# Products over 64 rows in place of 128 in half of a projection stage

## The chip, the core and the metric

The kernel runs on one core of one Trainium2 chip. The core has TensorE (PE for its products, PEld for its weight loads), VectorE (DVE), ScalarE (ACT), GpSimd (POOL) and SyncE (SP), a working memory of 128 partitions, and an accumulation memory (PSUM) in banks of 512 fp32 numbers per partition, of which the kernel uses all eight here. The metric is device time in microseconds (us) of one execution; lower is better.

## The reference

Two layers of an encoder over 2048 prompt tokens and 64 new ones, 1024 wide, 16 heads of 64. What matters here is the four-way and the two-way projection at the head of each layer:

```python
def a_project(x, g, w_in):
    h = rms_norm(x, g)
    q, k, v, gate = jnp.split(h @ w_in, 4, axis=-1)
    return split_heads(q), split_heads(k), split_heads(v), gate

def b_project(x, g, w_in):
    h = rms_norm(x, g)
    q, gate = jnp.split(h @ w_in, 2, axis=-1)
    return split_heads(q), gate

def shared_kv(x, g, w_kv):
    h = rms_norm(x, g)
    k, v = jnp.split(h @ w_kv, 2, axis=-1)
    return split_heads(k), split_heads(v)

def gated_out(o, gate, w_out):
    b, t = o.shape[:2]
    return (o.reshape(b, t, D_MODEL) * jax.nn.silu(gate)) @ w_out
```

Layer a then attends within a band of 64-token chunks with a softmax, layer b over all earlier tokens with a stick-breaking rule; each ends in `gated_out` and a residual, and a last norm follows. All inputs and outputs are fp32.

## The kernel before

**Numbers in two parts.** Every operand of a product is kept as a high part in fp32r and a low part that is the rest, and a product of two such operands is three products: high by high, high by low, low by high. `mm3` (line 227) does this: over the eight blocks of 128 input channels (`NK` = 8) it issues 24 matmuls into one bank. `split` (line 209) makes the two parts out of a bank: ACT copies it to fp32r, DVE subtracts that copy from the bank.

**The stages of the program.** Layer a: `projections` (line 239), then band attention with its output projection; layer b: `projections` again, then stick-breaking attention with its output projection. In the trace the two projection stages lie at about 0 to 800 us and 1500 to 2030 us.

**Inside `projections`.** First come the values (`ps_v`), token rows as output. Then the part that matters here: for each job (`q`, `k` or `g`, the gate) and each pair of heads (`hp`, eight of them) the weights of 128 output channels are loaded (`wraw`), scaled and split into `wh` and `wl`, and multiplied with the normed, transposed tokens. These lie in two places: the first 1088 (1024 prompt tokens and the 64 new ones) in `x_own`, high and low, and the second 1024 prompt tokens in the pair of tiles `big`. `HALVES` (line 57) cuts the first half in chunks of 364, 362 and 362 columns and the second (`hf` = 1) in two of 512. Each chunk is one `mm3` into one bank `ps_t` (line 395); the banks of this stage are five, under the tag `mm`, taken in turn. Gates leave the bank through a SiLU on ACT (`sg`), queries and keys through `split` (`sh`, `sl`), and DMAs store them.

**What is left for later.** `DEFER` (line 42) takes the second half of the keys out of layer a's stage and the second half of queries and gates out of layer b's. So the second half is projected here for 16 cases in layer a (`q` and `g`, eight pairs of heads each) and 8 in layer b (`k`), with two chunks each: 48 chunks, 1152 matmuls.

**What sets the order.** Most of the program is ordered by a scheduler that places instructions on the engines at build time; in parts of the attention the order is written out by hand (`Beat`). Work on caches and biases (`stages`) and the transposes that turn keys back to token rows (`natural`, bank `ps_n`; `stage_cache`, bank `ps_c`) is spread between the projections, in three further banks. Each engine then runs its own list in order.

All instructions are recorded through one helper, so all of them stand under line 90 in the profile; the tiles' names tell them apart.

Of the kernel before, what the change touches and what calls it, by code (L numbers as in the profile page):

```python
# [9 lines left out]
F32 = mybir.dt.float32  # L10
F32R = mybir.dt.float32r
AF = mybir.ActivationFunctionType
ALU = mybir.AluOpType
# [3 lines left out]
P = 128  # L17
D = 1024
NK = D // P
H = 16  # L20
DH = 64
# [11 lines left out]
CH = 512  # L33
# [27 lines left out]
def spot(r):  # L61

    return (0, NEW) if r == NP else divmod(r, HALF)
# [7 lines left out]
def f32(ap):  # L71
    return ap.bitcast(F32)
# [28 lines left out]
def encoder_step(ctx: ExitStack, tc: tile.TileContext, a: dict, o: dict):  # L101
    nc = tc.nc
    order = InOrder(tc)
    dve, act, gps, pe = (order.engine(x) for x in (nc.vector, nc.scalar, nc.gpsimd, nc.tensor))
    mm = pe.matmul
# [66 lines left out]
    for L, rows in (("a", CACHE_A), ("b", PAST)):  # L172
# [4 lines left out]
            k=[dram.tile([2, P, T + rows], F32R, name=f"k_{L}{i}") for i in range(HP)],  # L177
# [6 lines left out]
            w={x: dram.tile([2, P, NK, P], F32R, name=f"w_{L}{x[0]}{x[1]}") for x in DEFER[L] if L in KEPT},  # L184
# [24 lines left out]
    def split(hi, lo, src):  # L209
        act.activation(hi, src, AF.Copy)  # L210
        dve.tensor_tensor(lo, src, f32(hi), ALU.subtract)

    def scaled_split(hi, lo, src, g):
        for k in range(src.shape[1]):
            act.activation(hi[:, k], src[:, k], AF.Copy, scale=g[:, k : k + 1])
            dve.scalar_tensor_tensor(lo[:, k], src[:, k], g[:, k : k + 1], f32(hi[:, k]), ALU.mult, ALU.subtract)
# [10 lines left out]
    def mm3(out, sh, sl, mh, ml):  # L227
        for k in range(NK):
            mm(out, sh(k), mh(k), start=(k == 0), stop=False)
            mm(out, sh(k), ml(k), start=False, stop=False)  # L230
            mm(out, sl(k), mh(k), start=False, stop=(k == NK - 1))

    def put(L, kind, hp, s, cols, part, by=nc.sync.dma_start):

        for i in (0, 2) if kind == "q" and s == 0 else (s,):
            by(f32(lay[L][kind][hp][i, :, cols]), f32(part))


    def projections(L, x_of, begin, w_v, cv, gv, out_v, jobs, first, prompt, sample, stages):
        with (  # L240
# [7 lines left out]
            with tc.tile_pool(name=f"v_{L}", bufs=2) as pool:  # L248
# [54 lines left out]
                for half in range(2):  # L303
                    wh, wl = [], []
# [17 lines left out]
                    for i, t in enumerate(seq):  # L322
# [3 lines left out]
                        hf, c = spot(r0)  # L326
                        xh, xl = xs[hf]
                        ps = psum.tile([P, CH], F32, name="ps_v", tag="mm", bufs=5)
                        out = ps[:n]
                        if n == NS:  # L330
# [4 lines left out]
                            out = pool.tile([P, CH], F32, name="vn", tag="vn", bufs=2)[:n]  # L335
# [30 lines left out]
            with tc.tile_pool(name=f"st_{L}", bufs=5) as spool, tc.tile_pool(name=f"t_{L}", bufs=2) as pool:  # L366
                for j, (kind, w, c0, g) in enumerate(jobs):
                    for hp in range(HP):
                        for _ in range(-(-len(stages) // (len(jobs) * HP - j * HP - hp))):
                            stages.pop(0)(pool)  # L370

                        home, tag = (pool, "wr") if hp % 2 else (opool, "og")
                        raw = home.tile([P, NK, P], F32, name="wraw", tag=tag, bufs=1)
                        c = c0 + hp * P
                        wh = opool.tile([P, NK, P], F32R, name="wh", tag="oh", bufs=2)
                        wl = opool.tile([P, NK, P], F32R, name="wl", tag="ol", bufs=2)

                        with tc.issue_after(first_copy.ins) if j == 0 and hp < 2 else nullcontext():
                            nc.scalar.dma_start(raw, w[:, c : c + P].rearrange("(k p) c -> p k c", p=P))
                            scaled_split(wh, wl, raw, g)  # L380
                        if (kind, hp) in lay[L]["w"]:
                            for i, part in enumerate((wh, wl)):
                                nc.sync.dma_start(f32(lay[L]["w"][kind, hp][i]), f32(part))
                        for hf, (r0, n, chunks) in enumerate(HALVES):
                            xh, xl = xs[hf]
                            if hf and (kind, hp) in DEFER[L]:

                                continue
                            if kind == "g":
                                sg = spool.tile([P, 1088], F32, name="sg", tag="st")  # L390
                            else:
                                sh = spool.tile([P, 1088], F32R, name="sh", tag="st")
                                sl = spool.tile([P, 1088], F32R, name="sl", tag="st")
                            for c, m in chunks:
                                ps = psum.tile([P, CH], F32, name="ps_t", tag="mm", bufs=5)
                                mm3(
                                    ps[:, :m],
                                    lambda k: wh[:, k],
                                    lambda k: wl[:, k],
                                    lambda k: xh[:, k, c : c + m],  # L400
                                    lambda k: xl[:, k, c : c + m],
                                )
                                if kind == "g":
                                    act.activation(sg[:, c : c + m], ps[:, :m], AF.Silu)
                                else:
                                    split(sh[:, c : c + m], sl[:, c : c + m], ps[:, :m])
                            if kind == "g":
                                nc.sync.dma_start(lay[L]["g"][hp][:, r0 : r0 + n], sg[:, :n])
                                continue
                            for s, part in enumerate((sh, sl)):  # L410
                                put(L, kind, hp, s, slice(r0, r0 + n), part[:, :n])
                            if kind == "k":

                                cols = slice(hp * P, hp * P + P)
                                for c in range(0, HALF, CH):
                                    b = hf * HALF + c - first
                                    if b >= 0:
                                        kf = pool.tile([P, CH], F32, name="kf", tag="kf", bufs=2)
                                        part = slice(c, c + CH)
                                        gps.tensor_tensor(kf, f32(sh[:, part]), f32(sl[:, part]), ALU.add)  # L420
                                        natural(pool, kf, 0, P, 4, prompt[b : b + CH, cols])
                                if hf == 0:
                                    kf = pool.tile([P, CH], F32, name="kf", tag="kf", bufs=2)
                                    part = slice(NEW, NEW + NS)
                                    gps.tensor_tensor(kf[:, :NS], f32(sh[:, part]), f32(sl[:, part]), ALU.add)
                                    natural(pool, kf, 0, NS, 1, sample[:, cols])
# [82 lines left out]
    def natural(pool, kf, at, n, nt, dst):  # L509
        ps = bank("ps_n").rearrange("p (j c) -> p j c", j=4)  # L510
        for j in range(nt):
            flip(ps[:n, j], kf[:, at + j * n : at + j * n + n])
        kn = pool.tile([P, 4, P], F32, name="kn", tag="kn", bufs=2)
        act.activation(kn[:n, :nt], ps[:n, :nt], AF.Copy)
        nc.sync.dma_start(dst.rearrange("(j p) c -> p j c", p=n), kn[:n, :nt])
# [220 lines left out]
    def late_job(L, kind, w, c0, g, hp, x2, first, prompt):  # L736
# [27 lines left out]
        def out(c):  # L764
            ps = st["ps"]
            at = slice(place(HALF + c), place(HALF + c) + CH)
            if kind == "g":
                sg = opool.tile([P, CH], F32, name="sg", tag="xr", bufs=2)
                act.activation(sg, ps, AF.Sigmoid)
                dve.tensor_tensor(sg, ps, sg, ALU.mult)  # L770
                queue.store(lay[L]["g"][hp][:, at], sg)
            else:
                sp = opool.tile([P, 2, CH], F32R, name="sp", tag="xr", bufs=2)
                split(sp[:, 0], sp[:, 1], ps)
                for s in range(2):
                    put(L, kind, hp, s, at, sp[:, s], queue.store)
                st[c] = sp
            if c + CH == HALF:
                done_late.add((L, kind, hp))
# [307 lines left out]
    with (  # L1087
# [158 lines left out]
        ("q", a["w_in_b"][0], 0, gs["b"]),  # L1246
    ]
    x2 = projections(
        "b",
        x1_rows,  # L1250
# [12 lines left out]
    with (  # L1263
# [9 lines left out]
            out=own_s[:, CH - P :], in_=own_s[:, CH - P :], pattern=[[-1, P]], compare_op=ALU.is_gt,  # L1273
# [3 lines left out]
        for h in range(2):  # L1277
            rows = slice(h * DH, h * DH + DH)
# [267 lines left out]
```

## Time and profile before

| what | value |
|---|---|
| median of 2 runs | 3279.51 us (3278.79 and 3280.22) |
| span of the profiled execution | 3278.2 us |
| what lies around the span, by the two runs | 0.6 to 2.0 us |
| PE busy | 3204.2 us, 98% of the span |
| PEld, DVE, ACT, POOL busy | 85%, 58%, 52%, 39% |
| mean granted TensorE clock | 0.994 of full speed |

A group of instructions is written as line, engine, operation, output<-inputs, rows*columns of the weights, shape, count, then busy time and mean duration of one, then the idle time of the engine before them. A product's duration holds its way through the array, so products overlap: the pace is read from the distance between starts. In a timeline, rows of like neighbours are merged: start, time from the first start to the last end, and a count.

### The profile page before, as it was taken

Reading aid. Unit: us, or ns where it says so; the run is one execution under the profiler, and the core shown is the slowest. Engines: PE = TensorE matmul, PEld = TensorE weight load, DVE = VectorE, ACT = ScalarE, POOL = GpSimd, SP = SyncE. Lnnn points to the kernel's source line nnn. Section 1 sums busy time; section 2 is a strip of 40 time slices with the busy share of each in tenths; the row PEclk is TensorE's granted clock in tenths of the full one; section 3 lists DMA queues with packets and bytes.
Section 4 is the critical chain, followed back from the end, with each engine's and each line's share of the span. In section 5 each row is a group of like instructions: output and inputs, shape, how many; then the busy total and the mean of one; then the engine's idle time right before and its main releaser. Section 6 shows DMA issues by size and latency. Waiting matters only on the chain.

```text
span 3278.2 us, 53687 instructions
## 1 busy us (share of the span) xinstructions
PE 3204.2 (98%) x17928; PEld 2791.0 (85%) x17928; DVE 1887.0 (58%) x3786; ACT 1711.4 (52%) x3719; POOL 1291.4 (39%) x1950
## 2 busy tenths in 40 slices
PE   8999999999998999999999999999999989999999
PEld 7889999988887898878889998788888878888877
DVE  4235431147778775231044333788878878888873
ACT  5234222258888776143134442566666656666662
POOL 3001110026665554020044200444477766877761
PEclk9999999999999999999999999999999999999999
DMA  6359993387899983553399999977735566455423
GB/s 202 121 185 368 349 331 118 117 237 220 240 260 267 252 237 130 164 174 128 113 357 352 348 357 328 251 217 217 213 121 148 162 203 174 124 143 141 138 72 119
DMA packets 464892, 688.41 MB, mean 210 GB/s; under 512 B 51446, under 2 KB 261398, under 8 KB 464615
## 3 DMA queue, kind: packets, MB, share of 16 engines
q1 hardware_dynamic: 405158, 633.85, 61.8%
q10 hardware_dynamic: 59456, 51.13, 4.8%
q8 instruction: 143, 2.34, 0.3%
q14 instruction: 135, 1.10, 0.1%
HBM read 408.78 MB, written 276.07 MB: 209 GB/s over the span
## 4 chain that ended last, share of the span: by engine, by line
PE 75%; issue 7%; DVE 6%; DMA 6%; ACT 2%; POOL 2%; SPq 1%; POOLq 0%; ACTq 0%; DVEq 0%
PE ps_t L90 23%; PE ps_v L90 11%; PE acc L90 10%; PE z L90 9%; PE wt L90 8%; PE ps_j L90 6%; PE ps_o L90 5%; DVE s L90 3%; DVE pl L90 2%; DMA vt<-v_b 1%; PE ps_tr L90 1%; ACT ph L90 1%; DMA kt<-k_b 1%; POOL s L90 1%; ACT s L90 1%
## 5 line engine op out<-in xcount | busy, mean ns | idle before, releaser
L90 DVE TENSOR_TENSOR pl<-wt,ph 128x512 fp32r<-128x512 f32 (+1 forms) x864 | 551.9, 654 | 122.4 <-ACT ph L90 118.7
L90 ACT ACTIVATE ph<-wt 128x512 fp32r<-128x512 f32 (+1 forms) x864 | 485.7, 578 | 205.4 <-PE wt L90 178.2
L90 PE MATMUL ps_t<-x_own,wh 128*128 128x362 f32 (+1 forms) x2304 | 567.5, 327 | 0.0
L90 PE MATMUL wt<-ident,s 128*128 128x128 f32 x3472 | 551.5, 274 | 13.4 <-DVE pl L90 6.8
L90 PEld LDWEIGHTS wt<-ident,s 128*128 128x128 f32 x3472 | 418.6, 141 | 88.3 <-DVE pl L90 12.9
L90 ACT ACTIVATE f<-z 128x512 f32<-128x512 f32 (+4 forms) x680 | 355.1, 535 | 196.1 <-PE z L90 139.7
L90 PEld LDWEIGHTS ps_t<-x_own,wh 128*128 128x128 f32 x2304 | 405.0, 188 | 1.8
L90 POOL TENSOR_TENSOR s<-f,s 128x256 f32<-128x256 f32 x416 | 361.3, 870 | 104.2 <-DVE s L90 95.9
L90 PE MATMUL acc<-ph,vt 128*128 128x512 f32 (+3 forms) x1088 | 376.2, 381 | 14.1 <-DMA vt<-v_b 7.5
L90 PE MATMUL z<-kt,q 128*128 128x512 f32 (+3 forms) x1280 | 375.4, 381 | 12.9 <-DMA q<-q_b 5.8
L90 PE MATMUL ps_t<-x_own,wl 128*128 128x362 f32 (+1 forms) x1152 | 376.7, 327 | 0.0
L90 PE MATMUL acc<-pl,vt 128*128 128x512 f32 (+3 forms) x1088 | 364.6, 368 | 7.2 <-DVE pl L90 6.8
L90 POOL TENSOR_SCALAR s<-s,rc 128x640 f32<-128x640 f32 (+5 forms) x264 | 199.2, 760 | 387.3 <-DMA keys<-k_a 193.3
L90 PE MATMUL ps_o<-big,oh 128*128 128x512 f32 x1088 | 336.2, 392 | 0.2 <-ACT oh L90 0.2
L90 POOL TENSOR_TENSOR two<-f 128x256 f32<-128x256 f32 x416 | 259.5, 626 | 166.3 <-ACT f L90 150.0
L90 DVE TENSOR_TENSOR_SCAN s<-two,s,own 128x256 f32<-128x256 f32 x408 | 299.7, 738 | 33.6 <-POOL two L90 32.3
L90 PEld LDWEIGHTS z<-kt,q 128*128 128x128 f32 x1280 | 221.9, 192 | 43.5 <-ACT f L90 11.8
L90 PE MATMUL ps_j<-big,lwh 128*128 128x512 f32 x768 | 246.9, 397 | 1.1 <-DVE pl L90 0.6
L90 PE MATMUL ps_t<-big,wh 128*128 128x512 f32 x768 | 238.9, 391 | 0.0
L90 PEld LDWEIGHTS ps_o<-big,oh 128*128 128x128 f32 x1088 | 202.2, 188 | 41.3 <-ACT oh L90 0.4
L90 PEld LDWEIGHTS acc<-ph,vt 128*128 128x128 f32 x1088 | 198.7, 192 | 37.1 <-ACT ot L90 8.4
L90 DVE CUSTOM_DVE_ANT_0 s<-z,bias 128x640 f32<-128x640 f32 (+4 forms) x256 | 184.7, 733 | 77.2 <-PE wt L90 51.1
(148 smaller groups left out, 5528.9 us busy)
## 6 DMA issues: line engine op xcount, KB each, us to landing
vt<-v_b SPq DMA_DIRECT2D x80, 512.0 KB, 4.9
v_b<-vs SPq DMA_DIRECT2D x64, 512.0 KB, 5.7
q<-q_a SPq DMA_DIRECT2D x128, 256.0 KB, 5.9
q<-q_b SPq DMA_DIRECT2D x128, 256.0 KB, 4.6
vt<-v_a SPq DMA_DIRECT2D x48, 512.0 KB, 7.1
kt<-k_b SPq DMA_DIRECT2D x96, 256.0 KB, 5.6
keys<-k_a SPq DMA_DIRECT2D x80, 256.0 KB, 7.1
v_a<-vs ACTq DMA_DIRECT2D x32, 512.0 KB, 2.7
```

The source lines that it names most:

```text
L90: ins = op(*args, **kwargs)
```

## The change

For chunks of the second half (`hf` = 1), and only there, `mm3` is replaced by the new `by_rows`. It takes a second bank of the same five and issues each of the 24 products as two: one over partitions 0 to 63 of weights and tokens into the first bank, one over partitions 64 to 127 into the second. Weights are still 128 columns wide and tokens 512. When both sums are done, ACT copies the first bank to a tile in working memory (`total`, under the tag `kf` that the keys use too) and DVE adds the second bank to it. What followed reads `total` in place of the bank: SiLU for gates, `split` for queries and keys. The 48 chunks so have 2304 matmuls in place of 1152, 48 more ACT and 48 more DVE instructions; loads and stores are the same in number and size.

```diff
+    def by_rows(pool, psum, ps, wh, wl, xh, xl):
+
+        outs = [ps, psum.tile([P, CH], F32, name="ps_t", tag="mm", bufs=5)]
+        terms = [(w, x, k) for k in range(NK) for w, x in ((wh, xh), (wh, xl), (wl, xh))]
+        for i, (w, x, k) in enumerate(terms):
+            for r, out in enumerate(outs):
+                rows = slice(r * DH, r * DH + DH)
+                mm(out, w[rows, k], x[rows, k], start=(i == 0), stop=(i == len(terms) - 1))
+        total = pool.tile([P, CH], F32, name="total", tag="kf", bufs=2)
+        act.activation(total, outs[0], AF.Copy)
+        dve.tensor_tensor(total, outs[1], total, ALU.add)
+        return total
...
                             for c, m in chunks:
                                 ps = psum.tile([P, CH], F32, name="ps_t", tag="mm", bufs=5)
-                                mm3(
-                                    ps[:, :m],
-                                    lambda k: wh[:, k],
-                                    lambda k: wl[:, k],
-                                    lambda k: xh[:, k, c : c + m],
-                                    lambda k: xl[:, k, c : c + m],
-                                )
+                                if hf:
+                                    ps = by_rows(pool, psum, ps, wh, wl, xh[:, :, c : c + m], xl[:, :, c : c + m])
+                                else:
+                                    mm3(
+                                        ps[:, :m],
+                                        lambda k: wh[:, k],
+                                        lambda k: wl[:, k],
+                                        lambda k: xh[:, k, c : c + m],
+                                        lambda k: xl[:, k, c : c + m],
+                                    )
                                 if kind == "g":
                                     act.activation(sg[:, c : c + m], ps[:, :m], AF.Silu)
                                 else:
```

TensorE, at the end of the first chunk of the second half (layer a, queries) and the start of its second chunk, before; `big0` and `big1` are the tokens' high and low part, the number behind `ps_t` tells the bank's tile:

```order
1520 L90 MATMUL ps_t_3098<-big0_184,wh_2991 128x512
1521 L90 MATMUL ps_t_3098<-big1_185,wh_2991 128x512
1522 L90 MATMUL ps_t_3098<-big0_184,wl_2992 128x512
1523 L90 MATMUL ps_t_3125<-big0_184,wh_2991 128x512
1524 L90 MATMUL ps_t_3125<-big1_185,wh_2991 128x512
1525 L90 MATMUL ps_t_3125<-big0_184,wl_2992 128x512
```

The same place after the change:

```order
1541 L90 MATMUL ps_t_3098<-big0_184,wh_2991 128x512
1542 L90 MATMUL ps_t_3099<-big0_184,wh_2991 128x512
1543 L90 MATMUL ps_t_3098<-big1_185,wh_2991 128x512
1544 L90 MATMUL ps_t_3099<-big1_185,wh_2991 128x512
1545 L90 MATMUL ps_t_3098<-big0_184,wl_2992 128x512
1546 L90 MATMUL ps_t_3099<-big0_184,wl_2992 128x512
1547 L90 MATMUL ps_t_3153<-big0_184,wh_2991 128x512
1548 L90 MATMUL ps_t_3154<-big0_184,wh_2991 128x512
```

Each product now stands twice, first for partitions 0 to 63, then for 64 to 127, and the banks alternate from one instruction to the next. The pairs stay together in this way through the chunks; where a transpose (`ps_n`, `ps_c`) is placed among them, the products over 64 rows stop for it and go on behind it. Counted over the whole list, they stand in 43 unbroken stretches.

VectorE, at the same chunk's way out of its bank, before (`vs` and `bt` belong to the staged work, `wl` to the next weights):

```order
166 L90 TENSOR_TENSOR vs<-vprev,vs 128x8x64
167 L90 TENSOR_TENSOR sl<-ps_t,sh 128x512
168 L90 SCALAR_TENSOR_TENSOR wl<-wraw,g_a,wh 128x128 x2
169 L90 TENSOR_SCALAR bt<-toe 128x256
170 L90 TENSOR_SCALAR bt<-toe 128x384
171 L90 SCALAR_TENSOR_TENSOR wl<-wraw,g_a,wh 128x128 x2
```

And after the change:

```order
166 L90 TENSOR_TENSOR vs<-vprev,vs 128x8x64
167 L90 TENSOR_TENSOR total<-ps_t,total 128x512
168 L90 TENSOR_SCALAR bt<-toe 128x256
169 L90 TENSOR_SCALAR bt<-toe 128x384
170 L90 MEMSET bt 64x64 x2
171 L90 TENSOR_TENSOR sl<-total,sh 128x512
```

The add that empties the second bank stands where the subtraction stood, and the subtraction follows behind four instructions of staged work; the splitting of the next weights moves behind it.

## The prediction

> **What bounds the kernel now.** I read the page's totals and slices first, then the chain that ended last, then the groups.
>
> ```profile
> span 3278.2 us, 53687 instructions
> PE 3204.2 (98%) x17928; PEld 2791.0 (85%) x17928; DVE 1887.0 (58%) x3786; ACT 1711.4 (52%) x3719; POOL 1291.4 (39%) x1950
> PE   8999999999998999999999999999999989999999
> PE ps_t L90 23%; PE ps_v L90 11%; PE acc L90 10%; PE z L90 9%; PE wt L90 8%; PE ps_j L90 6%; PE ps_o L90 5%; DVE s L90 3%; DVE pl L90 2%; DMA vt<-v_b 1%; PE ps_tr L90 1%; ACT ph L90 1%; DMA kt<-k_b 1%; POOL s L90 1%; ACT s L90 1%
> L90 PE MATMUL ps_t<-big,wh 128*128 128x512 f32 x768 | 238.9, 391 | 0.0
> ```
>
> TensorE is busy in every slice, and the chain that sets the end runs through `ps_t` for 23% of the span. The group that the change touches (768 products with `wh` and half as many with `wl`) has no idle time before it: nothing is waited for, so each nanosecond that a product gains or loses here moves the end by as much.
>
> What the other engines do in the stages concerned comes from the busy times of three stretches, layer a's projections of queries and gates in two parts and layer b's of keys and the rest:
>
> ```profile
> core 0: us, PE busy (x) PEld busy (x) DVE busy (x) ACT busy (x) POOL busy (x), PEclk, DMA share, GB/s
> 212.00:505.00 293.00, 291.82 (x1650) 275.88 (x1650) 128.17 (x323) 103.48 (x270) 46.26 (x43) 1.00 0.96 339
> 505.00:800.00 295.00, 287.35 (x1599) 258.09 (x1597) 107.62 (x309) 126.87 (x311) 58.39 (x70) 0.99 0.54 165
> 1620.00:2030.00 410.00, 408.78 (x2394) 387.50 (x2392) 160.14 (x324) 160.41 (x391) 90.94 (x74) 1.00 0.96 344
> ```
>
> DVE and ACT are at 35 to 44%, and the granted clock is at 0.99 to 1.00. TensorE alone is the bound.
>
> How fast the products go is read from the timeline of PE (start, length, count) in the first chunks of the second half:
>
> ```profile
> 327.52 0.62 PE L90 MATMUL ps_t<-big,wh 128*128 128x512 f32 x2
> ...
> 328.65 0.39 PE L90 MATMUL ps_t<-big,wl 128*128 128x512 f32 x1
> 328.88 0.62 PE L90 MATMUL ps_t<-big,wh 128*128 128x512 f32 x2
> 329.33 0.39 PE L90 MATMUL ps_t<-big,wl 128*128 128x512 f32 x1
> ...
> 335.45 0.39 PE L90 MATMUL ps_t<-big,wl 128*128 128x512 f32 x1
> ```
>
> From 327.52 to 335.45 lie 12 groups of three less the last product, 35 distances: 7.93 / 35 = 0.227 us from one start to the next. The loads of their weights, from PEld's timeline:
>
> ```profile
> 328.65 0.41 PEld L90 LDWEIGHTS ps_t<-big,wh 128*128 128x128 f32 x2
> 329.11 0.19 PEld L90 LDWEIGHTS ps_t<-big,wl 128*128 128x128 f32 x1
> ```
>
> The load for the product that starts at 328.88 begins at 328.65, with the product before it. Loads are hidden under products over all 128 rows.
>
> **The change part by part.**
>
> *The products: 0 if the two of a pair run side by side.* 1152 products of 0.227 become 1152 pairs. Each half still passes 512 columns, so neither can be expected below 0.227, and a pair side by side costs what the one product cost: the array was full before and is full after. A pair cannot win time; it can only lose it. No pair on different rows is in this trace, so the cost lies between 0.227 (side by side) and 2 x 0.227 = 0.454 (one after the other). I take the lower end. For it speaks that the halves share neither rows of weights, nor rows of tokens, nor a bank.
>
> What else a pair needs is two weight loads. How close loads can follow each other shows where products are short, the sample's 128-column products of fp32r:
>
> ```profile
> 1005.12 1.19 PEld L90 LDWEIGHTS acc<-pp,vt 128*128 128x128 f32 x10 [0.21 <-ACT ot L90]
> ```
>
> Ten loads in 1.19, the last one 0.19 long: nine distances of 0.111. Two loads are 0.222, just under 0.227. So loads of a pair still fit beneath it, with 0.005 to spare. If loads were the pace, a pair would cost 0.222: 1152 x 0.005 = 6 us less than now, the lowest end I can give.
>
> *Going in and out of 64 rows: +15.5 us.* The trace has the transposes of the 64 new tokens, which are work over 64 rows, and the same transposes over 128 rows shortly before. First the lengths of one (min/median/max in ns), then the timeline around both visits:
>
> ```profile
> L90 PE MATMUL ps_tr<-ident,xt x272: 221/272/476, 7.1 to 1511.6; 128*128 128x128 f32 x128, 64*128 64x64 f32 x8
> L90 PEld LDWEIGHTS ps_tr<-ident,xt x272: 135/140/230, 7.1 to 1511.6; 128*128 128x128 f32 x128, 64*128 64x128 f32 x8
> ```
>
> ```profile
> 97.29 0.39 PE L90 MATMUL ps_v<-vwh,big 128*128 128x512 f32 x1
> 97.52 1.04 PE L90 MATMUL ps_tr<-ident,xt 128*128 128x128 f32 x8
> 98.31 0.47 PE L90 MATMUL ps_v<-vwh,big 128*128 128x512 f32 x1
> 98.63 0.39 PE L90 MATMUL ps_v<-vwl,big 128*128 128x512 f32 x1
> ...
> 103.74 0.40 PE L90 MATMUL ps_v<-vwh,big 128*128 128x512 f32 x1
> 104.07 0.71 PE L90 MATMUL ps_tr<-ident,xt 64*128 64x64 f32 x8
> 104.70 0.50 PE L90 MATMUL ps_v<-vwh,big 128*128 128x512 f32 x1
> 105.04 0.39 PE L90 MATMUL ps_v<-vwl,big 128*128 128x512 f32 x1
> 104.06 0.57 PEld L90 LDWEIGHTS ps_tr<-ident,xt 64*128 64x128 f32 x8 [0.37 <-issue]
> ```
>
> With 128 rows: from the product at 97.29 to the second one behind the transposes, 98.63, are 1.34 us; two products at 0.23 and eight transposes at (1.04 - 0.27) / 7 = 0.11 make 1.34, so the visit is free. With 64 rows: 103.74 to 105.04 are 1.30, of which products are 0.46 and eight transposes, by the distance of their loads (0.57 - 0.14) / 7 = 0.06, 0.49; 0.35 to 0.36 are left over. That is what one visit to 64 rows and back costs. The products over 64 rows stand in 43 stretches: 43 x 0.36 = 15.5 us. Ends: 0, if those transposes lost it to something of their own, and 43 x (0.36 + 0.11) = 20 us, if the second row group's first load shows as well.
>
> *The way out: 0, but for one tail of 1.3 us.* Per chunk ACT has one more copy of 128x512 and DVE one more pass:
>
> ```profile
> L90 ACT ACTIVATE sh<-ps_t 128x512 fp32r<-128x512 f32 x16 | 9.4, 587 | 38.6 <-PE ps_t L90 38.6
> L90 DVE TENSOR_TENSOR sl<-ps_t,sh 128x512 fp32r<-128x512 f32 x16 | 11.1, 692 | 37.8 <-ACT sh L90 36.9
> ```
>
> 48 x (0.587 + 0.692) = 61 us on engines that are 35 to 44% busy in stages of some 1000 us together; TensorE covers it. The cover has a limit: five banks. A pair of chunks takes four, the next three chunks of the first half one each, and both banks of a chunk are free 1.28 us after its last product, if DVE's add is not held up behind other work. The next chunk takes 24 x 0.227 = 5.4 us and uses other banks, so the cover is four times the need. Where a stage ends in such a chunk (layer a's last gate), the 1.28 show once. The later subtraction and the weight splits moved behind it have the time of a whole pair of heads. Loads and stores stay as they are.
>
> *Sum.* 3278.2 + 0 + 15.5 + 1.3 = 3295.0 for a profiled execution; the median of the runs stands 1.3 above the span, so 3296 us.
>
> **The rivals.**
>
> *One after the other (slower).* If the two halves don't overlap, each of the 1152 pairs costs 0.454: +261.5 us, 3278.2 + 261.5 + 15.5 + 2.6 = 3558 (2.6 are the tail and what the median stands above the span). For it: no row here shows two products at once, and the 64-row transposes of one row group follow each other at 0.06 without overlap. Against: those share their rows, the pairs don't. It decides from 0.268 per pair on, where (0.268 - 0.227) x 1152 + 18 reach 2%. That the change doesn't do what it says would be the same case.
>
> *Half hidden.* If the second product, or the next pair, has to wait for one load of 0.111, a pair costs 0.338: +128 us, 3424. Against it: in the 64-row row above, loads run ahead of their products, eight at a distance of 0.06. The Trainium skill, "TensorE: Matmul & The Clock Gate", Part 3, gives four products on four row groups as 3.07 times as fast, not four times. As an estimate from that page, a pair would cost 0.227 x 4 / 3.07 = 0.296 and the kernel 3376; no run here shows a pack yet.
>
> *Loads laid bare now, hidden then (faster).* If each product now paid for its load, alternating row groups would hide 1152 x 0.111 = 128 us: 3278.2 - 128 + 15.5 + 2.6 = 3168. The Trainium skill (same page, Part 3, "What overlaps and what doesn't") says that loads overlap with running products only where the row groups differ. By that rule this case would hold; the rows at 328.65 contradict it, since a load over the same 128 rows begins with the product before its own.
>
> *Banks run out.* Were TensorE to wait for each chunk's copy and add, 48 x 1.28 = 61 us: 3358. It starts where a bank is held longer than 5.4 us, and ACT and DVE idle times above (37 to 39 us before 16 such instructions) speak against it.
>
> **How the numbers follow.** Side by side 0.66, one after the other 0.18, half hidden 0.13, faster 0.02, banks 0.01. The predicted time is that of the first. Its own bounds are 3278.2 - 6 + 1.3 = 3274 and 3278.2 + 20 + 2.6 = 3301. To leave out no more than 2 in 10, the range goes from 3274 through banks and half hidden to 3425; the serial and the faster case are outside. 2% of the median (66 us) is about what a measurement tells from no change: faster 0.02; within it 0.66; slower 0.18 + 0.13 + 0.01 = 0.32.
>
> **What would show it.** Right: in the timeline after, the two products of a pair start within 0.11 of each other and pairs follow at 0.22 to 0.24; around each stretch some 0.36 are lost; `ps_t` still has no idle time before it. Of the 43 stretches 17 are in layer a and 26 in layer b, so the first two windows above grow by some 6 us and the third by some 9. Wrong: 2304 evenly spaced products at 0.227 (one after the other), a spacing near 0.34 per pair (half hidden), or idle time of PE before `ps_t` with ACT or DVE `total` as its releaser (banks).

## The result and the profile after

The changed kernel takes 3389.05 us (3388.11 to 3389.98, 2 runs) against 3279.51 before: 1.033 times as long, with a 95% interval of 1.030 to 1.036. It is slower by 109.5 us, where 16.5 were forecast. The page of the changed kernel, in the parts that were shown of before:

```profile
span 3386.3 us, 56063 instructions
PE 3243.9 (96%) x19080; PEld 2807.6 (83%) x19080; DVE 1908.3 (56%) x3834; ACT 1741.6 (51%) x3767; POOL 1296.0 (38%) x1950
PE 67%; DMA 10%; issue 8%; DVE 7%; ACT 4%; POOL 3%; SPq 1%; POOLq 0%; ACTq 0%; DVEq 0%
L90 PE MATMUL ps_t<-big,wh 64*128 64x512 f32 x1536 | 260.0, 399 | 16.3 <-ACT total L90 12.5
```

The third line has the shares of the chain that ended last. Before, it read:

```profile
PE 75%; issue 7%; DVE 6%; DMA 6%; ACT 2%; POOL 2%; SPq 1%; POOLq 0%; ACTq 0%; DVEq 0%
```

TensorE's part falls from 75% to 67%, and that of DMA rises from 6% to 10%. The last line of the page above shows that the group the change touches no longer runs without waiting: 16.3 us of idle time stand before it, 12.5 of them ended by ACT's `total`.

The products themselves are not at fault. PE's timeline in the first chunk of the second half (start, length, engine, operation, count):

```profile
328.07 0.83 PE L90 MATMUL ps_t<-big,wh 64*128 64x512 f32 x4
328.53 0.60 PE L90 MATMUL ps_t<-big,wl 64*128 64x512 f32 x2
328.75 0.83 PE L90 MATMUL ps_t<-big,wh 64*128 64x512 f32 x4
```

From 328.07 to 328.75 lie six products, three pairs: 0.68 / 3 = 0.227 us per pair, what one product over 128 rows took. The two of a pair start 10 ns apart in this chunk, and 3 to 4 ns apart in most others.

So where do 108 us of span come from? I compared where each pair of heads starts: the start of its first product in the trace of after, less that of before. These are the starts of layer a's third and seventh query pair, of layer b's first key pair, and of the pair behind its last key pair, before and then after:

```profile
358.27 0.50 PE L90 MATMUL ps_t<-x_own,wh 128*128 128x364 f32 x2
448.64 0.50 PE L90 MATMUL ps_t<-x_own,wh 128*128 128x364 f32 x2
1620.08 0.49 PE L90 MATMUL ps_t<-x_own,wh 128*128 128x364 f32 x2
1823.11 0.50 PE L90 MATMUL ps_t<-x_own,wh 128*128 128x364 f32 x2
...
358.85 0.60 PE L90 MATMUL ps_t<-x_own,wh 128*128 128x364 f32 x2
482.63 0.60 PE L90 MATMUL ps_t<-x_own,wh 128*128 128x364 f32 x2
1656.78 0.50 PE L90 MATMUL ps_t<-x_own,wh 128*128 128x364 f32 x2
1939.52 0.60 PE L90 MATMUL ps_t<-x_own,wh 128*128 128x364 f32 x2
```

The delay is 0.6 us at the third query pair of layer a, 34.0 at its seventh and 37.6 at the last gate; 36.7 at the first pair of key heads of layer b, 116.4 behind the eighth; 108.1 at the end. **Some 33 us are lost in four pairs of query heads, some 80 in eight pairs of key heads, and nearly nothing elsewhere;** 8 are won back behind them, by the end of the span. In the gates, where the same products run, each pair of heads adds 0.4.

TensorE's waits in the two stretches of after (time in total, how often, the longest), layer a's first:

```profile
PE ps_t L90 <- ACT total L90: 17.5, 7, 7.7
PE ps_t L90 <- DVE total L90: 2.6, 3, 1.4
...
PE ps_n L90 <- POOL kf L90: 43.0, 11, 7.1
PE ps_c L90 <- DMA kr<-in_cache_b_k: 9.0, 4, 4.5
```

In layer a TensorE waits for banks to be emptied; in layer b its transposes of keys (`ps_n`) wait for the sum of high and low part that GpSimd makes (`kf`), and those of the cache (`ps_c`) for their load. What ACT waited for between 324 and 500 us says why the banks are full; before, and then after:

```profile
ACT sh L90 <- PE ps_t L90: 84.8, 26, 5.0
...
ACT vs L90 <- POOL vprev L90: 86.2, 22, 10.2
ACT sh L90 <- PE ps_t L90: 10.0, 4, 3.4
```

Before, ACT spent this stretch waiting for TensorE to finish a bank, which costs nothing. After, it waits as long for *staged work*, the differences of the cache's values that GpSimd makes and ACT splits (`vs`). ACT works through its list in order, so a finished bank waits too. All engines at one such place in after, in order of time:

```profile
372.87 1.26 POOL L90 TENSOR_TENSOR vprev<-vprev,vcur 128x512 f32<-128x512 f32 x1 [7.67 <-DMA vprev<-in_cache_b_v]
374.17 0.63 ACT L90 ACTIVATE vs<-vprev 128x512 fp32r<-128x512 f32 x1 [7.78 <-POOL vprev L90]
375.87 0.57 ACT L90 ACTIVATE total<-ps_t 128x512 f32<-128x512 f32 x1
376.50 0.79 PE L90 MATMUL ps_t<-big,wh 64*128 64x512 f32 x1 [4.39 <-ACT total L90]
```

A load lands, GpSimd subtracts, ACT splits, ACT copies a bank that its products had left some 17 us before, and only then does TensorE get that bank: 4.39 us idle. Most such waits are followed by slow products: of the 13 waits of 2.7 us or longer in the two stretches, 11 have the clock at half in them or right behind them. Granted clock (`PEclk`, the third figure from the end) and DMA's share (the last but one) in such stretches of after, and in two whole pairs of heads before:

```profile
375.00:382.00 7.00, 4.06 (x17) 2.90 (x19) 6.59 (x17) 4.24 (x12) 3.21 (x2) 0.52 0.90 297
1914.50:1924.70 10.20, 5.74 (x22) 5.74 (x23) 5.37 (x12) 5.34 (x12) 2.54 (x2) 0.51 1.00 355
...
380.00:403.00 23.00, 23.00 (x123) 21.03 (x122) 9.19 (x24) 6.52 (x16) 3.06 (x3) 1.00 1.00 353
1671.00:1697.00 26.00, 25.77 (x144) 22.97 (x143) 9.92 (x18) 9.71 (x22) 11.28 (x10) 1.00 0.95 343
```

In all there are 20.4 us at half the clock in layer a's projections and 47.6 in layer b's keys, where before had none. Not all of it counts, since the half clock often begins within the wait: in the first line above TensorE is busy for 4.06 of 7.00 us. Over all of these stretches it is busy for 13.5 us in layer a and 32.9 in layer b, and about half of that is lost, 6.7 and 16.4 us. The stretches are 3.4, 6.8 or 10.2 us long. The Trainium skill ("TensorE: Matmul & The Clock Gate", Part 1) names a free-running window of about 3.4 us after which an idle TensorE is taken to half its clock; the lengths agree, but a wait as short as 2.73 us was followed by half the clock here as well.

In layer a, 21.3 us of waits (17.5, 2.6 and one of 1.2) and 6.7 of slow clock, with 0.4 for each of four visits, make 29.6 of the 33.4 measured between the third and the seventh query pair; what the other 3.8 are was not followed. In layer b, 52.3 us of waits and 16.4 of slow clock, with 0.36 for each of 26 visits, make 78.1 of the 79.7. Before has about 1 us of waits there.

Why more staged work than ACT can take? Not since there is more in all, but since its place in the list has moved. ACT's list at the chunks of one pair of query heads (in the traces at 344 to 359 and at 352 to 376 us), before:

```
217 L90 ACTIVATE vs<-vprev 128x8x64
218 L90 ACTIVATE sh<-ps_t 128x362
219 L90 ACTIVATE sh<-ps_t 128x512
220 L90 ACTIVATE vs<-vprev 128x8x64
221 L90 ACTIVATE wh<-wraw,g_a 128x128 x4
222 L90 ACTIVATE sh<-ps_t 128x512
```

and after:

```
221 L90 ACTIVATE vs<-vprev 128x8x64
222 L90 ACTIVATE sh<-ps_t 128x362
223 L90 ACTIVATE vs<-vprev 128x8x64
224 L90 ACTIVATE total<-ps_t 128x512
225 L90 ACTIVATE vs<-vprev 128x8x64
226 L90 ACTIVATE sh<-total 128x512
227 L90 ACTIVATE vs<-vprev 128x8x64
228 L90 ACTIVATE wh<-wraw,g_a 128x128 x4
229 L90 ACTIVATE total<-ps_t 128x512
```

Before, one staged split at most stands between two emptyings of banks, and often none; after, one stands ahead of nearly each. The order of the lists is laid down when the program is built. Counted from one pair of heads to the next, the splits on ACT's list (`vs` from `vprev` or `vcur`) are:

| kernel | layer a, pairs of query heads | layer b, pairs of key heads |
|---|---|---|
| before | 3, 3, 3, 2, 3, 3 | 4, 3, 3, 4, 3, 4, 4, 4 |
| after | 4, 6, 6, 7, 4, 0 | 5, 7, 6, 7, 6, 9, 9, 1 |

How fast these pieces can come is seen in the differences that GpSimd makes from 324 to 500 us, before and after (count, length min/median/max in ns, first and last start):

```profile
L90 POOL TENSOR_TENSOR vprev<-vprev,vcur x25: 1284/1292/1802, 332.3 to 498.6; 128x512 f32<-128x512 f32 x25
...
L90 POOL TENSOR_TENSOR vprev<-vprev,vcur x26: 1262/1292/2332, 322.7 to 467.1; 128x512 f32<-128x512 f32 x26
```

After, with ACT waiting for them, they come (467.1 - 322.7) / 25 = 5.8 us apart. A pair of query heads took 22.6 us of TensorE: 3.9 pieces. The list of before asks for 2 or 3, that of after for 4 to 7. The DMA engines, which bring the pieces, have little to spare. Their share is the last figure but one, first before, then after:

```profile
324.00:470.00 146.00, 146.00 (x770) 132.86 (x769) 56.73 (x133) 41.51 (x102) 25.07 (x19) 1.00 0.95 339
...
324.00:470.00 146.00, 124.69 (x835) 108.87 (x835) 54.85 (x122) 41.85 (x95) 34.34 (x26) 0.93 0.92 329
```

My theory from here, **"order"**: the build lays the other engines' work among the products as if each of the 2304 took its turn alone, so staged work is put among half as many pairs as it needs; on the chip the pairs run side by side, and everything that was laid beside them is late. What times the build assumes is not on record; only its lists are. The rivals: **"banks"** (two banks and a long way out for each chunk), **"rows"** (64-row products cost more than they show, among other work), **"buffers"** (`total` shares its two tiles with `kf`).

### The profile page after: what moved, and what is told of

It reads as the page before. It is cut to its first block, busy times and chain, and to the rows that moved or that the text cites. A ratio compares the mean times of both kernels' runs of the same rounds, so it can differ in the third digit from the quotient of the medians.

```text
span 3386.3 us, 56063 instructions
## 1 busy us (share of the span) xinstructions
PE 3243.9 (96%) x19080; PEld 2807.6 (83%) x19080; DVE 1908.3 (56%) x3834; ACT 1741.6 (51%) x3767; POOL 1296.0 (38%) x1950
## 4 chain that ended last, share of the span: by engine, by line
PE 67%; DMA 10%; issue 8%; DVE 7%; ACT 4%; POOL 3%; SPq 1%; POOLq 0%; ACTq 0%; DVEq 0%
PE ps_t L90 17%; PE ps_v L90 11%; PE acc L90 10%; PE z L90 9%; PE wt L90 8%; PE ps_j L90 6%; PE ps_o L90 5%; DVE s L90 3%; DVE pl L90 2%; DMA vprev<-v_raw 2%; DMA vprev<-in_cache_b_v 2%; DMA vt<-v_b 1%; DMA vcur<-in_w_out_b 1%; ACT ph L90 1%; POOL vprev L90 1%
## 5 line engine op out<-in xcount | busy, mean ns | idle before, releaser
L90 PE MATMUL ps_t<-x_own,wh 128*128 128x362 f32 (+1 forms) x2304 | 577.2, 332 | 5.0 <-ACT total L90 5.0
L90 PE MATMUL ps_t<-big,wh 64*128 64x512 f32 x1536 | 260.0, 399 | 16.3 <-ACT total L90 12.5
L90 PEld LDWEIGHTS acc<-pl,vt 128*128 128x128 f32 x1088 | 194.4, 190 | 40.1 <-DVE pl L90 24.6
```

What stands on the lines that cost most here:

```text
L90: ins = op(*args, **kwargs)
```

## The experiments

Each time stands beside runs of the kernel before on the same chip, 3278.4 to 3280.5 us.

**1. Two banks and the long way out, with products over 128 rows.** The products of a chunk go to the two banks in turn; copy and add are as in the changed kernel.

```diff
-            for r, out in enumerate(outs):
-                rows = slice(r * DH, r * DH + DH)
-                mm(out, w[rows, k], x[rows, k], start=(i == 0), stop=(i == len(terms) - 1))
+            mm(outs[i % 2], w[:, k], x[:, k], start=(i < 2), stop=(i >= len(terms) - 2))
```

> Two banks per chunk, ACT copy and DVE add on the way out as in the change, but products over all 128 rows (24 per chunk, in turn into the two banks). Theory 'order' (the scheduler counts 2304 products over 64 rows as twice the time, lays about twice as much staged work per pair of heads on ACT ahead of the copies that empty the banks, and the chip waits for that work's loads): here the count of products is as before, ACT's list has 2 to 4 staged splits per pair of heads as before and not 6 to 7, so 3279 to 3290 us. Rival 'banks' (half the cover of five banks and the longer way out cost it whatever the order): 3350 to 3390. Rival 'rows' (the products over 64 rows themselves, or switching to them): 3279 to 3285.

Measured: 3276.84 us, ratio 0.9995 (0.9986 to 1.0004). The 48 copies and adds are there, and cost nothing:

```profile
L90 ACT ACTIVATE total<-ps_t x48: 579/598/622, 329.5 to 1824.6; 128x512 f32<-128x512 f32 x48
L90 DVE TENSOR_TENSOR total<-ps_t,total x48: 674/691/693, 330.2 to 1825.2; 128x512 f32<-128x512 f32 x48
```

TensorE has no wait between 324 and 500 us, and the list of ACT is nearly that of before (3, 2, 4, 2, 3, 3 splits; 4, 3, 3, 4, 3, 4, 4, 3). "Banks" falls as a cause by itself, and it is the 48 products of a chunk, not its way out, that move the lists.

**2. 64 rows for the gates alone.** In the gates of layer a hardly any staged splits are left.

```diff
-                                if hf:
+                                if hf and L == "a" and kind == "g":
```

> The change for layer a's gates alone: 16 of 48 chunks, 384 of 1152 pairs, eight visits to 64 rows; no staged work with slow loads stands in this part. 'Order' and 'banks': 8 x 0.4 us, which is what a pair of heads of gates gained in the trace after (22.6 to 23.0), so 3282 to 3284. 'Rows': a third of 110 us, 3316.

Measured: 3283.61 us, ratio 1.0020 (1.0011 to 1.0028), 5.2 us more and in the range of "order" and "banks", TensorE without any wait between 330 and 700 us. Eight pairs of heads add 0.4 each. From the last projection to the first product of the attention (`z`) there are 13.3 us in place of 9.4, but TensorE never idles there: 58 of the products left for later (`ps_j`) stand ahead of `z`, where before has 42. So the tail of 1.3 us that was forecast for the end of layer a cannot be seen as a wait.

**3. The order alone, in the kernel before.** Products over 128 rows, one bank. At each pair of heads 5 pieces of staged work are called (layer a, from the queries on) or 8 (layer b), and the emptying of the second half's banks is put behind it on ACT's list: 8, 5, 5, 5, 3, 1 and 7, 6, 7, 7, 7, 8, 3, 5 splits. `cut` lists ACT's part of each split.

```diff
...
+                        share = len(stages) / (len(jobs) * HP - j * HP - hp)
+                        full = L == "b" or j == 1
+                        for _ in range(min(len(stages), dict(a=5, b=8)[L] if full else int(share + 0.999))):
                             stages.pop(0)(pool)
+                        staged_act = cut[-1] if full and cut else None
...
+                                    with tc.issue_after(staged_act.ins) if staged_act and hf else nullcontext():
+                                        split(sh[:, c : c + m], sl[:, c : c + m], ps[:, :m])
```

> The kernel before, one bank per chunk and products over 128 rows, with the staged work of the stage called at 5 (layer a, from the queries on) and 8 (layer b) pieces per pair of heads and ACT's emptying of the second half's banks put behind it, so that ACT's list has 5 to 8 staged splits per pair of heads, as dense as after the change. 'Order': 3340 to 3390 without any product over 64 rows and without a second bank. 'Banks' and 'rows': 3279 to 3295.

Measured: 3381.31 us, ratio 1.0313 (1.0299 to 1.0327). The loss is there, in size and in the two stretches, with no product over 64 rows and no second bank: the delay is 44.7 at the seventh query pair, 120.5 behind the key heads, 105.2 at the end. TensorE's waits differ in name:

```profile
PE ps_c L90 <- DMA kr<-in_cache_b_k: 72.1, 15, 9.9
PE ps_t L90 <- DVE sl L90: 12.1, 6, 7.1
```

It waits mostly for the cache's keys. In the first seven pairs of key heads 12, 12, 16, 12, 20, 16 and 8 of their transposes stand on TensorE's list, where the changed kernel has 12, 8, 4, 8, 4, 8 and 4, so layer b's order is denser here in this respect. The run shows that order alone can cost as much; that the two sums come out nearly alike is in part chance, and the waits of the changed kernel are others.

**4. Three buffers for `total` and `kf`** in the changed kernel (`bufs=2` to `bufs=3`).

> The whole change, with three buffers instead of two for the tag that `total` shares with `kf`; order of the staged work as in the changed kernel. 'Order': 3380 to 3392, no change that counts. Rival 'buffers' (the sums and the keys' natural copies wait for one another's two buffers, and TensorE for both): 3300 to 3350.

Measured: 3389.09 us, ratio 1.0342 (1.0326 to 1.0358), as the changed kernel. "Buffers" falls.

**5. The whole change with the staged work held back.** The work called at a pair of heads may not stand on ACT's list before the last emptying of a bank of the pair before; in layer b it is called for at 1.8 times its even share (the pieces left over the pairs of heads left), which makes up for the hold. `emptied` is ACT's last instruction that read a bank.

```diff
...
+                        share = len(stages) / (len(jobs) * HP - j * HP - hp)
+                        for _ in range(min(len(stages), int(share * dict(a=1.0, b=1.8)[L] + 0.999))):
+                            with tc.issue_after(emptied.ins) if emptied else nullcontext():
+                                stages.pop(0)(pool)
```

> The whole change, with 64-row pairs, two banks and the long way out; only the staged work of a pair of heads is put behind the last emptying of the pair of heads before it on ACT's list (in layer b 1.8 times as much is called per pair of heads, so that it isn't left for the end). ACT's list has 2 to 5 staged splits per pair of heads in place of 6 to 9. 'Order': most of the loss goes, 3290 to 3315 (43 visits at 0.36 = 15 us stay). 'Banks' and 'rows': 3370 to 3390.

Measured: 3331.39 us, ratio 1.0165 (1.0150 to 1.0181), with 4, 5, 2, 2, 2, 2 and 3, 5, 3, 3, 2, 3, 2, 2 splits. More than half the loss is gone with every product as in the changed kernel, but it is 16 us above the top of what was expected. What is left of waits among the key heads has one name:

```profile
PE ps_c L90 <- DMA kr<-in_cache_b_k: 16.9, 7, 5.0
```

The transposes of the cache are staged work as well. In the first seven pairs of key heads, 16, 12, 12, 8, 12, 8 and 12 of them now stand on *TensorE's* own list, ahead of their loads; before has 12, 8, 4, 8, 0, 8 and 4.

**6. and 7. Fewer of them**, with 1.2 and 1.4 times the even share.

> The run before this one (whole change, staged work of a pair of heads held behind the last emptying of the pair before on ScalarE's list) left 35 us more than the 15 of the 64-row visits, and its trace shows the waits of the rest at `ps_c <- kr`: the cache's transposes stand in TensorE's list ahead of their loads, 12 to 16 of them in each pair of key heads of layer b where the kernel before has 0 to 12 (8, 4, 8, 0, 8, 4 after the first). Here the same hold is kept and the staged work of layer b is called for 1.2 times its even share instead of 1.8, which makes 8 of these transposes in each pair of key heads; the products are the same. 'Order': the waits on `kr` shrink and the time falls below the run before it, to 3300 to 3325. 'Rows' (what is left is the price of the 64-row products themselves among staged work): 3325 to 3337, as there. A price at the end for staged work that now comes after the last pair of heads (13 splits there) is possible and would be seen in the last delay, not among the key heads.

> The same with 1.4 times the even share in layer b (8 to 12 of the cache's transposes in each pair of key heads, 9 staged splits after the last pair of heads instead of 13). 'Order': between the run with 1.8 (3331) and the one with 1.2. 'Rows': 3325 to 3337.

Measured: 3337.25 us (ratio 1.0184, 1.0169 to 1.0199) and 3334.87 (1.0172, 1.0153 to 1.0191): no gain, against what "order" expected. By the times alone "rows" would have won here. The traces say more: the delay behind the key heads falls from 52.8 to 34.1 and 43.4, and then the next stage's first products wait for keys and values of layer b that are stored too late, in the run with 1.2 first:

```profile
PE z L90 <- DMA kt<-k_b: 32.8, 2, 32.3
...
PE z L90 <- DMA vt<-v_b: 27.1, 1, 27.1
```

Staged work has a latest time as well as an earliest one.

**8. The hold in the kernel before** (128 rows, one bank, 1.8 times the share).

> The kernel before (128 rows, one bank) with the hold of the paced run and its 1.8 shares in layer b: what the hold itself costs or gives when no product is in 64 rows. 'Order': 3278 to 3300; whatever it costs over 3278 is to be taken off the paced run's loss. 'Rows': the same, 3275 to 3285, since no product is changed.

Measured: 3290.87 us, ratio 1.0041 (1.0026 to 1.0055). The hold itself costs 12 us. If the two add, 40 of the paced run's 53 are left for the products and their order.

**9. and 10. A written list**, in the changed kernel and in the kernel before: at each pair of heads as many staged pieces are called, and held as above, as ACT's list has in before (`V_B` and `K_B` are values and cache keys of layer b).

```diff
...
+V_B = [4, 3, 3, 4, 3, 4, 4, 4, 1, 2, 1, 1, 2, 2, 2, 1, 2, 1, 2, 1, 1, 0, 1, 1]
+K_B = [2, 2, 1, 2, 0, 2, 1, 1, 1, 1, 1, 1, 1, 1, 1, 1, 1, 1, 1, 1, 1, 0, 0, 0]
+PLAN = dict(a=[3, 3, 3, 3, 4, 0, 2, 2, 1, 3, 3, 3, 2, 3, 3, 4, 4, 2, 2, 2, 2, 1, 1, 0], b=[v + k for v, k in zip(V_B, K_B)])
...
+                        for _ in range(len(stages) if last else min(len(stages), PLAN[L][j * HP + hp])):
+                            with tc.issue_after(emptied.ins) if emptied else nullcontext():
+                                stages.pop(0)(pool)
```

> The whole change again, with the staged work called by a written list: for each pair of heads as many staged value splits as stand on ScalarE's list in the kernel before (layer a from the seventh pair on 2, 1, 1, 3, 3, 3, 3, 2, 3, 3, 4, 4, layer b 6, 3, 3, 4, 3, 4, 4, 3, 2, 1, ... against 2, 2, 1, 3, 3, 3, 2, 3, 3, 4, 4, 2 and 4, 3, 3, 4, 3, 4, 4, 4, 1, 2, ... before), held behind the last emptying of the pair before. The cache's transposes of layer b come in about the same places as before too. The evenly paced runs left 35 to 40 us more than the visits: partly since work called evenly was missing later (the next stage then waited 27 to 33 us for its first loads), partly since layer a still had 4 and 5 splits in two pairs of heads. 'Order': 3294 to 3312, the 15.5 us of the visits and at most a few waits, no wait of the next stage's first products for their keys over 8 us. 'Rows' (what the paced runs kept is a price of the 64-row products among staged work): 3325 to 3340, as in those.

> The same written list in the kernel before (128 rows, one bank), as the other side of the run above: what the list itself costs or gives. 'Order': 3275 to 3290, since the list is nearly that of the kernel before; the difference of the two runs is then what the 64 rows cost when the order is alike, 14 to 20 us. 'Rows': 3275 to 3290 too, and a difference of 40 to 60 us.

Measured: 3323.73 us (ratio 1.0134, 1.0115 to 1.0153) and 3289.74 (1.0033, 1.0022 to 1.0045), a difference of 34: more than "order" allowed, less than "rows" asked. The first time is 12 us above the range of "order" and 1 below that of "rows".

**11. and 12. A second list** that starts smaller in layer b (`V_B` from 2, 3, 3, 4, `K_B` from 1, 2, 1, 2, and some pieces of layer a later), again in both kernels.

> The first written list took 34 us more than the same list at 128 rows, 18 to 20 beyond the visits, and its trace puts 17 us of that in the first two pairs of key heads of layer b (delay 10.9 at the start of the first, 27.7 at the start of the third), where 6 splits and 12 of the cache's transposes stood in the first pair against 4 and 12 in the kernel before, and a wait of 5.2 us for `kr` was followed by half the clock. Here the list starts smaller there: 4, 3, 3, 4, 3, 4, 4, 4 splits and 8, 8, 4, 8, 4, 4, 4 transposes of the cache in the pairs of key heads, the same amount of work in all; in layer a one split fewer in some pairs. 'Order': the growth over those first two pairs falls from 17 to under 8 and the time to 3300 to 3315. 'Rows' (64-row products among staged work cost this by themselves): 3318 to 3330, as with the first list.

> The second written list in the kernel before (128 rows, one bank): the other side of the run before this one (3317), with ScalarE's staged splits alike in nearly every pair of heads (3, 4, 3, 4, 3, 4, 4, 3 in the pairs of key heads against 4, 3, 3, 4, 3, 4, 4, 4) and the cache's transposes in the same places. The difference of the two is what the 64 rows cost at a like order. 'Order', with the visits at their 15.5: 3288 to 3302, a difference of 15 to 29. 'Rows' (a price of the 64-row products beyond the visits, among staged work): 3278 to 3286, a difference of over 30.

Measured: 3316.98 us (ratio 1.0115, 1.0098 to 1.0132) and 3287.25 (1.0018, 1.0008 to 1.0028). The growth over the first two pairs of key heads falls from 17 to 7 us, as expected; the time is 2 us above the range of "order" and 1 below that of "rows". The difference of the two is 30 us, on the border between the theories, so the times don't decide. Where it lies says more. Starts compared pair by pair between these two runs, layer a adds 8.4: 0.4 at nearly each pair and 2.7 at one, where TensorE waits 1.8 for `DVE total`. Layer b adds 24.6 by its second pair of gate heads, among which the last keys are turned. TensorE's waits there, first at 64 rows, then at 128:

```profile
PE ps_n L94 <- POOL kf L94: 9.3, 7, 3.2
...
PE ps_n L94 <- POOL kf L94: 0.7, 1, 0.7
```

24 visits at 0.36 are 8.6, the waits 8.6 more, and of 10.2 us at half the clock, which begin within the two longest (3.0 and 3.2), TensorE is busy for 8.8 and loses 4.4: 21.6 of the 24.6. And why the transposes wait, at the same place of the two runs, 64 rows first (`ps_n` twice, the second time for 5 transposes of the next keys):

```profile
1642.74 0.60 PE L94 MATMUL ps_n<-ident,kf 128*128 128x128 f32 x4
1649.23 1.33 PE L94 MATMUL ps_n<-ident,kf 128*128 128x128 f32 x5 [2.96 <-POOL kf L94]
...
1635.57 0.60 PE L94 MATMUL ps_n<-ident,kf 128*128 128x128 f32 x4
1641.35 0.76 PE L94 MATMUL ps_n<-ident,kf 128*128 128x128 f32 x5
```

Between the two stand 23 products over 128 rows, 23 x 0.227 = 5.2 us, and no wait; or 23 over 64 rows, which are 11.5 pairs and 2.6 us, and a wait of 2.96. So at this place TensorE's own list has its transposes laid by the number of products too. That the rest would go if they stood twice as far apart is argued from this and was not run, so a small price of the 64-row products of their own, up to the 3 us that are left, is not ruled out.

The delays against before, in us, side by side:

| at the start of | after | 3, dense before | 5, paced | 9, list | 11, second list | 12, the same, 128 rows |
|---|---|---|---|---|---|---|
| layer a, seventh query pair | 34.0 | 44.7 | 12.6 | 7.8 | 4.5 | -0.2 |
| layer a, last gate | 37.6 | 40.9 | 16.2 | 12.4 | 9.1 | 0.7 |
| layer b, first key pair | 36.7 | 41.9 | 14.8 | 10.9 | 9.3 | 1.6 |
| layer b, behind the key pairs | 116.4 | 120.5 | 52.8 | 41.4 | 29.2 | 1.7 |
| the span's end | 108.1 | 105.2 | 46.9 | 42.9 | 34.9 | 7.0 |

No run with 64 rows beats the kernel before: 3283.61 with the gates alone is the least.

## Why the prediction was right in part, and what failed

**The products: right.** Pairs follow at 0.227 us. "One after the other" and "half hidden" are out, and so is a gain from laid-bare loads. The Trainium skill's 3.07 times for four row groups, from which 3376 was estimated, doesn't hold for two row groups here; its span model (same page, Part 3, "Measured speedup vs the span model": one product plus some 4 ns for each further tile) does, with starts 3 to 4 ns apart in most pairs. That the total came near 3376 is chance.

**Going in and out of 64 rows: right.** 0.36 a visit was forecast; where nothing else is late, each pair of gate heads adds 0.4.

**The way out: right in its price.** Two banks, copy and add cost nothing where the order is as before (first experiment). The tail of 1.3 us is in no trace as a wait of TensorE, which has other products to run at layer a's end.

**The step that failed** is the end of the part on the way out: "The later subtraction and the weight splits moved behind it have the time of a whole pair of heads. Loads and stores stay as they are." and, with it, the cover "four times the need", on the condition that "DVE's add is not held up behind other work". The number and size of the loads did stay. Their place against the products did not, and the condition was broken on ACT, one engine earlier: the copy stood behind staged work, 9 to 21 us behind the end of its chunk in the bad stretch. The add was held up as well, but TensorE waited only 2.6 us for it. The prediction looked at VectorE's list at one place, and saw staged work there; it didn't count that work over a stretch, on ACT's list and TensorE's. The sum so lacks one term: some 73 us by the spans, the 108.1 of the changed kernel less the 34.9 that stay with the second list and every product unchanged.

A sign of it stood in the prediction's own table. From 35 to 44% busy time of DVE and ACT and from the clock it concludes "TensorE alone is the bound", and passes over the DMA share: 0.96 in the two stretches that later lost time, 0.54 in the one that lost next to nothing. Where loads already fill the DMA engines, work that is asked for earlier need not come earlier. That the DMA share is what sets the limit was not tested in a run of its own.

**The rival "banks run out"** had the right sign in layer a and the right mark in the profile, idle time of PE before `ps_t` with ACT `total` as its releaser. But its mechanism was 1.28 us of work per chunk; what held the banks was a queue. Its argument against, long idle times of ACT, was read off a list that the change replaced: an engine with 38 us of idle time before such instructions still serves late if the next item in its list is not ready.

**The windows** were to grow by 6 us in layer a and 9 in layer b. They grew by 37 and 80. With the second list layer a grows by 9, and layer b's key pairs by 20.

**The range** reached as far as 3389 for rivals that didn't take place; the cause that did was in none of the cases. That the measured time lies inside it is luck.

## What to carry to other kernels

When a build step lays out the order of several engines, a change to the number of instructions on one of them can change the lists of all the others: compare the lists engine by engine, count the items that depend on loads between two emptyings of a bank, and hold that rate against the rate at which the loads land. Idle time of an in-order engine is no cover unless the items ahead in its list are ready. Work that runs side by side on the chip but is written as two instructions needs its neighbours placed by time, not by count, and held work has a latest time too, or the next stage waits for it.

## What the runs showed of the hardware

Two products over 64 rows each, on the two halves of the rows and into two banks, run fully side by side: 0.227 us for the pair, 3 to 4 ns between their starts in most pairs. TensorE's waits cost about a third as much again by the clock, which was at half for 3.4 to 10.2 us in or behind 11 of the 13 waits of 2.7 to 7.7 us: 73.6 us of waits in the two stretches drew 23.1 more. Both halves into one bank was not run, so whether the second bank is needed at all stays open.
